# The mixer of a hybrid decoder: GpSimd's arithmetic goes to VectorE, and the cache's loads go from SyncE's queue to GpSimd's

## The chip, the core and the metric

One core of a Trainium2 chip runs the kernel. Its engines are TensorE (matrix products; "PE", its weight loads "PEld"), VectorE ("DVE"), ScalarE ("ACT"), GpSimd ("POOL") and SyncE ("SP", which in this kernel only issues transfers). Each engine executes its own queue in order; 16 DMA engines carry all transfers between the memory of the chip (HBM) and the on-chip memory (SBUF, 128 partitions). TensorE writes its sums to PSUM, which GpSimd cannot read. The metric is device time in microseconds (us) for one execution of the whole kernel, the median of several runs.

## The reference, cut to what matters

One layer of a hybrid decoder in float32, for a prompt of 256 tokens and, in the same pass, 8 decoded sequences ("batches") of 8 tokens each with a past of 2048 positions. All 320 tokens go through a half FFN, the mixer, and another half FFN.

```
h = ffn_half(x, ...)                              # x + 1/2 (silu(n Wg) * (n Wu)) Wd
z = rmsnorm(h) @ w_in                             # columns: q | k | v | a | b, 1024 each
q, k = rope(rmsnorm(q)), rope(rmsnorm(k))         # 16 heads of 64
u = a * sigmoid(b)
conv = silu(layernorm(causal_depthwise(u, 31 taps) + bias))
attn = mixture of 3 dilated windows: (128, every 1), (512, every 4), (2048, every 16)
h = h + concat(attn, conv) @ w_out
y = ffn_half(h, ...)
```

For the decoded tokens the attention reads keys and values from a cache of 2048 rows of 4 KB per batch; the windows need 512 near rows and, of the far ones, eight rows out of every sixteen. The conv of a decoded token reads 30 earlier rows of its state.

## The kernel before

**Layout.** Features lie on the partitions, the 320 tokens in the free dimension. A weight matrix is read in pieces of row tiles x 256 columns. Each piece is split in two for precision: wh, the high half (a cast on ScalarE, L238), and wl, the rest (raw - wh on VectorE, L239). `gemm` then runs three products per row tile, wh with the high half of the activations (L299), wh with the low half (L300), wl with the high half (L301). So TensorE can't finish a piece before ScalarE and VectorE have made its halves; there are three buffers for each half and four or five for the raw piece, which SyncE loads (L276) three pieces ahead in the mixer.

**Order.** The program is traced once, and a scheduler with a timing model of its own turns the trace into one fixed queue per engine. Work beside a gemm is traced between its pieces: `after` calls `pump`, which advances the attention of the decoded tokens (`sample`) by a fraction of a step per piece (RATE_K 0.55 beside the k products, RATE 1.05 beside conv and v, RATE_O 1.6 beside the output products), and takes NBG = 5 items per piece off `bg`, the conv's background list. `defer` traces something a few pieces later.

**Stages of the mixer.** q products; k products (the cache steps begin here); conv products c, four times two gemms (a and b); v products; the output projection's conv half with the prompt's attention beside it (o); then its attention half.

**Decoded tokens.** For each batch, `far_scores` takes six far tiles: it loads kf (128 cache rows x 1024, L511), multiplies it by qr, a copy of the batch's queries on all partitions (GpSimd, L512; qr is loaded at L507, one buffer), and sums each head's 64 products (VectorE, L513). `far_sums` spreads the sums with a mask (GpSimd, L520). `near_scores` loads four near tiles kn (L534), transposes them on TensorE and multiplies. `soft` is the softmax; its last steps are GpSimd's: z is cleared and filled (L568, L569) and px spread (L571). `values` loads ten value tiles vn (L610, VB = 3 buffers) and accumulates the products in PSUM (L614). kf has three buffers, kn two. All these loads are issued by SyncE, in the queue of the weights.

**Conv.** Per channel tile `conv_taps` lays 31 taps on `bg`: 21 on VectorE, each one instruction that multiplies and adds (L714 the first, L716 the others), and PTAPS = 10 as a product on ScalarE (L721, cprod) which GpSimd adds into csum (L725; the first is csum itself) and at the end to the rest (L749). `stap` does the decoded tokens in two halves: all windows times all taps on GpSimd (L734, into a buffer of kf), summed on VectorE (L736), the bias on ScalarE (L738). `norm_add` sums channel tiles, the even ones on VectorE, the odd ones on GpSimd (L808, L810); `act` halves its products in the same way (L839).

**q and k.** `qk_norm` runs two of its products on GpSimd (L447, L455) and GpSimd's copies to qsT and ksT (L458); conv's gate product is L791.

## Time and profile before

| | |
|---|---|
| median of 3 runs | 2650.08 us (2642.70 to 2655.48) |
| span of the profiled execution, from its first to its last instruction | 2650.1 us |
| instructions | 43147 |
| PE, PEld busy | 2536.2 us (96%), 2424.5 us (91%) |
| DVE busy | 1445.5 us (55%) |
| ACT busy | 1031.1 us (39%) |
| POOL busy | 447.6 us (17%), 392 instructions |
| DMA | 443.21 MB, 167 GB/s in the mean |
| cache loads | 80 vn, 48 kf, 32 kn, 512 KB each |

The profiled execution's own time is known as its span alone. A share of busy time is a mean over the whole span, in which FFN 1, the mixer and FFN 2 have different limits, so it is read by stage. "L301" is line 301 of the kernel; a group of instructions is named by its line, engine, operation and tiles (result <- operands). A wait is idle time of an engine, put down to what ended it. Matmuls are pipelined, and a busy PE isn't at its peak.

### The profile page before, as it was taken

The numbers are of one execution on the slowest core, as the hardware profiler recorded it, in microseconds if no ns is written. First come the engines' busy times: TensorE is split into PE (matmuls) and PEld (weight loads), VectorE is DVE, ScalarE is ACT, GpSimd is POOL, SyncE is SP. The second block draws the span as 40 slices with busy tenths as digits, with TensorE's granted clock in tenths as the row PEclk, the third lists the DMA queues.
The fourth block names the chain that finished last, engine by engine and source line by source line (L and its number), as shares of the span: only waits on it lengthen the run. The fifth ranks groups of instructions, "written<-read, shape, count | busy, mean of one in ns | idle before, by whom it ended". The sixth has DMA issues, their size and how long they took to land. (4 is left out here: it accounts for less than half of the span.)

```text
span 2650.1 us, 43147 instructions
## 1 busy us (share of the span) xinstructions
PE 2536.2 (96%) x17612; PEld 2424.5 (91%) x17612; DVE 1445.5 (55%) x1785; ACT 1031.1 (39%) x1597; POOL 447.6 (17%) x392
## 2 busy tenths in 40 slices
PE   7999999999999999888878899999999999999999
PEld 6999999999999998777666675999999999999999
DVE  5444444444444576979899744644444444444443
ACT  4333333333323456555434434533333333333333
POOL 3000000000000123746666400200000000000000
PEclk9999999999999999899989899999999999999999
DMA  6544444444444455978888966454444444544443
GB/s 191 162 151 151 147 149 151 151 151 149 149 149 151 151 156 166 237 217 232 232 216 232 259 186 185 146 153 150 151 152 148 151 149 149 151 151 150 148 150 119
DMA packets 385543, 443.21 MB, mean 167 GB/s; under 512 B 17274, under 2 KB 362290, under 8 KB 385328
## 3 DMA queue, kind: packets, MB, share of 16 engines
q1 hardware_dynamic: 385344, 440.45, 56.1%
q8 instruction: 138, 2.26, 0.4%
q14 instruction: 61, 0.50, 0.1%
HBM read 432.39 MB, written 8.71 MB: 166 GB/s over the span
## 5 line engine op out<-in xcount | busy, mean ns | idle before, releaser
L239 DVE TENSOR_TENSOR wl<-raw,wh 128x1024 fp32r<-128x1024 f32 (+1 forms) x736 | 868.6, 1182 | 933.9 <-ACT wh L238 921.7
L238 ACT CAST wh<-raw 128x1024 fp32r<-128x1024 f32 (+1 forms) x736 | 688.0, 936 | 1275.8 <-PE acc L300 1088.0
L299 PE MATMUL acc<-xh_a,wh 128*128 128x320 f32 x1408 | 437.2, 311 | 1.5 <-ACT wh L238 1.5
L300 PE MATMUL acc<-xl_a,wh 128*128 128x320 f32 x1408 | 437.4, 311 | 0.0
L301 PE MATMUL acc<-xh_a,wl 128*128 128x320 f32 x1408 | 436.9, 310 | 0.0
L301 PE MATMUL acc<-hh,wl 128*128 128x320 f32 x1408 | 435.5, 309 | 0.0
L299 PE MATMUL acc<-xh_c,wh 128*128 128x320 f32 x1408 | 435.3, 309 | 0.0
L300 PE MATMUL acc<-xl_c,wh 128*128 128x320 f32 x1408 | 435.1, 309 | 0.0
L301 PE MATMUL acc<-xh_c,wl 128*128 128x320 f32 x1408 | 435.1, 309 | 0.0
L300 PE MATMUL acc<-hl,wh 128*128 128x320 f32 x1408 | 435.0, 309 | 0.0
L299 PE MATMUL acc<-hh,wh 128*128 128x320 f32 x1408 | 435.0, 309 | 0.0
L348 POOL TENSOR_TENSOR hm<-ut,sg 128x320 f32<-128x320 f32 x88 | 77.4, 880 | 1659.5 <-DVE ut L346 1659.5
L299 PEld LDWEIGHTS acc<-xh_a,wh 128*128 128x128 f32 x1408 | 265.9, 189 | 1.7 <-ACT wh L238 1.6
L300 PEld LDWEIGHTS acc<-xl_a,wh 128*128 128x128 f32 x1408 | 266.0, 189 | 0.3 <-issue 0.2
L301 PEld LDWEIGHTS acc<-xh_a,wl 128*128 128x128 f32 x1408 | 265.8, 189 | 0.5 <-DVE wl L239 0.2
L300 PEld LDWEIGHTS acc<-xl_c,wh 128*128 128x128 f32 x1408 | 264.4, 188 | 0.1
L299 PEld LDWEIGHTS acc<-xh_c,wh 128*128 128x128 f32 x1408 | 264.4, 188 | 0.1
L301 PEld LDWEIGHTS acc<-xh_c,wl 128*128 128x128 f32 x1408 | 264.4, 188 | 0.0
L300 PEld LDWEIGHTS acc<-hl,wh 128*128 128x128 f32 x1408 | 264.3, 188 | 0.0
L301 PEld LDWEIGHTS acc<-hh,wl 128*128 128x128 f32 x1408 | 264.3, 188 | 0.0
L299 PEld LDWEIGHTS acc<-hh,wh 128*128 128x128 f32 x1408 | 264.2, 188 | 0.0
L301 PE MATMUL acc<-xh_b,wl 128*128 128x320 f32 x640 | 205.5, 335 | 42.3 <-DVE wl L239 42.3
(214 smaller groups left out, 3016.5 us busy)
## 6 DMA issues: line engine op xcount, KB each, us to landing
raw<-ffn_w_gate SPq DMA_DIRECT2D x176, 512.0 KB, 3.6
raw<-ffn_w_up SPq DMA_DIRECT2D x176, 512.0 KB, 3.5
raw<-ffn_w_down SPq DMA_DIRECT2D x176, 512.0 KB, 3.5
vn<-cache_v SPq DMA_DIRECT2D x80, 512.0 KB, 6.6
raw<-w_in SPq DMA_DIRECT2D x128, 256.0 KB, 4.6
kf<-cache_k SPq DMA_DIRECT2D x48, 512.0 KB, 8.7
kn<-cache_k SPq DMA_DIRECT2D x32, 512.0 KB, 6.8
raw<-w_out SPq DMA_DIRECT2D x64, 256.0 KB, 5.0
```

Source lines behind the costliest of these rows:

```text
L238: nc.scalar.copy(dsth, src)
L239: nc.vector.tensor_tensor(dstl, src, dsth.bitcast(F32), op=ALU.subtract)
L299: nc.tensor.matmul(a, h, hi[kk], start=st, stop=False)
L300: nc.tensor.matmul(a, h, lo[kk], start=False, stop=False)
L301: nc.tensor.matmul(a, l, hi[kk], start=False, stop=sp)
L348: nc.gpsimd.tensor_tensor(m, t, sg[j], op=ALU.mult)
```

## The change

In the mixer GpSimd computes nothing any more. Its products (cache rows by queries, L512; conv windows, L734; the spreads L520 and L571; q's and k's L447 and L455; the gate L791; half of the layer norm's) go to VectorE as they are. Of the conv's taps VectorE does 30 of 31, and the first (with the bias) goes to ScalarE; cprod, csum and their adds are gone. `norm_add` keeps one sum, on VectorE, and its first copy goes to ScalarE; so do the copies to qsT, ksT and z. z becomes two fixed buffers that are cleared once. GpSimd issues the loads of kf, kn and vn instead of SyncE; qr, the weights and all stores stay with SyncE. The conv's window products are put after taps 6 and 14 instead of 3 and 9. GpSimd's work in the FFNs (L176, L348) and a few clears are untouched.

```diff
-PTAPS = 10
...
-            nc.gpsimd.tensor_tensor(zq, zq, sd, op=ALU.mult)
+            nc.vector.tensor_tensor(zq, zq, sd, op=ALU.mult)
...
-            nc.gpsimd.tensor_tensor(rot, rot, sin, op=ALU.mult)
+            nc.vector.tensor_tensor(rot, rot, sin, op=ALU.mult)
...
-            nc.gpsimd.tensor_copy((qsT if is_q else ksT)[:, i, :], r[:, SEQ:T])
+            nc.scalar.copy((qsT if is_q else ksT)[:, i, :], r[:, SEQ:T])
...
+    zbuf = deque(sa.tile([P, 2 * TS - TD], F32, name=f"z{i}", bufs=1) for i in range(2))
+    for z in zbuf:
+        nc.vector.memset(z, 0.0)
...
     def far_scores(b, out):
...
-            nc.sync.dma_start(kn, rows(ck, b, n))
-            nc.gpsimd.tensor_tensor(kn, kn, qr, op=ALU.mult)
+            nc.gpsimd.dma_start(kn, rows(ck, b, n))
+            nc.vector.tensor_tensor(kn, kn, qr, op=ALU.mult)
...
-        nc.gpsimd.tensor_tensor(af, bc(sf), tmb, op=ALU.mult)
+        nc.vector.tensor_tensor(af, bc(sf), tmb, op=ALU.mult)
...
-            nc.sync.dma_start(kn, rows(ck, b, NFAR + n))
+            nc.gpsimd.dma_start(kn, rows(ck, b, NFAR + n))
...
-        z = sa.tile([P, 2 * TS - TD], F32, name="z")
-        nc.gpsimd.memset(z, 0.0)
-        nc.gpsimd.tensor_copy(z[:, TS - TD:TS], sm[:, SNEW:SFAR])
+        z = turn(zbuf)
+        nc.scalar.copy(z[:, TS - TD:TS], sm[:, SNEW:SFAR])
...
-        nc.gpsimd.tensor_tensor(px, bc(sm[:, SFAR:SW]), tmb, op=ALU.mult)
+        nc.vector.tensor_tensor(px, bc(sm[:, SFAR:SW]), tmb, op=ALU.mult)
...
-                nc.sync.dma_start(v, rows(cv, b, vrow[n]))
+                nc.gpsimd.dma_start(v, rows(cv, b, vrow[n]))
...
     def conv_taps(i, u):
...
             if j == 0:
-                nc.vector.tensor_scalar(ap, src, w, bias, op0=ALU.mult, op1=ALU.add)
+                nc.scalar.activation(ap, src, AF.Identity, bias=bias, scale=w)
             else:
                 nc.vector.scalar_tensor_tensor(ap, src, w, ap, op0=ALU.mult, op1=ALU.add)
 
-        def ptap(j):
-            first = "c" not in s2
-            t = turn(csum if first else cprod)[:, 0:SEQ]
-            nc.scalar.activation(t, u[:, j:j + SEQ], AF.Copy, bias=0.0, scale=dww[:, i, j:j + 1])
-            if first:
-                s2["c"] = t
-            else:
-                nc.gpsimd.tensor_tensor(s2["c"], s2["c"], t, op=ALU.add)
...
-            nc.gpsimd.tensor_tensor(pr4, win, w, op=ALU.mult)
+            nc.vector.tensor_tensor(pr4, win, w, op=ALU.mult)
...
-        nd = CW - PTAPS
-        for j in range(nd):
+        for j in range(CW):
             bg.append(lambda j=j: tap(j))
-            k = (j + 1) * PTAPS // nd - j * PTAPS // nd
-            for x in range(k):
-                bg.append(lambda x=j * PTAPS // nd + x: ptap(nd + x))
-            if j in (3, 9):
-                bg.append(lambda j=j: stap(j > 3))
-        def close():
-            nc.gpsimd.tensor_tensor(ap, ap, s2["c"], op=ALU.add)
-            norm_add("m", a, i)
-
-        bg.append(close)
+            if j in (6, 14):
+                bg.append(lambda j=j: stap(j > 6))
+        bg.append(lambda: norm_add("m", a, i))
...
-            nc.gpsimd.tensor_tensor(uc, at[j], t, op=ALU.mult)
+            nc.vector.tensor_tensor(uc, at[j], t, op=ALU.mult)
...
-        e = nc.gpsimd if i % 2 else nc.vector
-        k = key + str(i % 2)
-        if i < 2:
-            norm[k] = tmp.tile([P, T], F32, name="n" + k, tag=("ssa", "sd")[i % 2], bufs=1)
-            e.tensor_copy(norm[k], x)
+
+        if i == 0:
+            norm[key] = tmp.tile([P, T], F32, name="n" + key, tag="ssa", bufs=1)
+            nc.scalar.copy(norm[key], x)
         else:
-            e.tensor_tensor(norm[k], norm[k], x, op=ALU.add)
+            nc.vector.tensor_tensor(norm[key], norm[key], x, op=ALU.add)
...
-            (nc.gpsimd if i % 2 else nc.vector).tensor_tensor(cacc[i], cacc[i], s["r"], op=ALU.mult)
+            nc.vector.tensor_tensor(cacc[i], cacc[i], s["r"], op=ALU.mult)
```

## Rows read from the trace of the kernel before

**Rows 1.** The page's slices, TensorE: busy tenths, 40 equal slices of the span.
```profile
PE   7999999999999999888878899999999999999999
```

**Rows 2.** Stretches: length, busy us of PE, PEld, DVE, ACT, POOL, clock, DMA share, GB/s.
```profile
1024.00:1118.00 94.00, 82.69 (x533) 74.85 (x532) 74.37 (x73) 51.95 (x109) 55.04 (x39) 0.91 0.91 246
1118.00:1349.00 231.00, 195.16 (x1562) 163.00 (x1560) 205.17 (x262) 118.39 (x264) 144.44 (x121) 0.94 0.81 223
1349.00:1492.00 143.00, 109.26 (x812) 87.92 (x811) 123.57 (x144) 63.01 (x138) 85.30 (x59) 0.88 0.93 238
1492.00:1616.00 124.00, 117.79 (x901) 90.14 (x900) 67.17 (x159) 45.53 (x113) 17.98 (x12) 0.97 0.75 205
...
1437.00:1500.00 63.00, 48.05 (x324) 39.72 (x325) 45.91 (x54) 29.69 (x62) 33.63 (x20) 0.87 1.03 256
```

**Rows 3.** Waits of TensorE, 1024 to 1492: total us, times, longest.
```profile
PE acc L301 <- DVE wl L239: 42.3, 25, 4.7
```

**Rows 4.** Groups of VectorE, 1024 to 1492: xcount | busy us, mean ns | idle before, releasers.
```profile
L716 DVE SCALAR_TENSOR_TENSOR cacc<-u,dww,cacc 128x256 f32<-128x256 f32 x160 | 134.3, 867 | 0.6
L239 DVE TENSOR_TENSOR wl<-raw,wh 128x512 fp32r<-128x512 f32 x126 | 124.7, 996 | 22.7 <-ACT wh L238 20.7 <-ACT kt L497 2.0
...
L457 DVE TENSOR_TENSOR qk<-w,w 128x320 f32<-128x320 f32 x11 | 9.2, 839 | 1.7 <-POOL w L455 1.7
...
L714 DVE TENSOR_SCALAR cacc<-u,dww,gains 128x256 f32<-128x256 f32 x8 | 7.6, 944 | 2.1 <-ACT u L792 2.1
L839 DVE TENSOR_TENSOR cacc<-cacc,mu 128x320 f32<-128x320 f32 x4 | 5.1, 1321 | 0.0
```

**Rows 5.** Timeline of VectorE: start us, us, what; successive instructions overlap a little.
```profile
1222.68 1.26 DVE L716 SCALAR_TENSOR_TENSOR cacc<-u,dww,cacc 128x256 f32<-128x256 f32 x3
1223.86 0.68 DVE L239 TENSOR_TENSOR wl<-raw,wh 128x512 fp32r<-128x512 f32 x1
1224.46 1.26 DVE L716 SCALAR_TENSOR_TENSOR cacc<-u,dww,cacc 128x256 f32<-128x256 f32 x3
```

**Rows 6.** Timelines of GpSimd and VectorE, 1208 to 1227.
```profile
1208.40 2.37 POOL L512 TENSOR_TENSOR kf<-kf,qr 128x1024 f32<-128x1024 f32 x1
...
1208.90 2.16 DVE L716 SCALAR_TENSOR_TENSOR cacc<-u,dww,cacc 128x256 f32<-128x256 f32 x1
...
1226.81 0.91 POOL L749 TENSOR_TENSOR cacc<-cacc,csum 128x256 f32<-128x256 f32 x1 [5.93 <-DVE cacc L716]
```

**Rows 7.** Groups of VectorE, 200 to 800, in FFN 1.
```profile
L239 DVE TENSOR_TENSOR wl<-raw,wh 128x1024 fp32r<-128x1024 f32 x171 | 215.5, 1260 | 285.0 <-ACT wh L238 285.0
```

**Rows 8.** Groups of GpSimd, 1024 to 1492.
```profile
L512 POOL TENSOR_TENSOR kf<-kf,qr 128x1024 f32<-128x1024 f32 x43 | 109.2, 2545 | 60.1 <-DMA qr<-dqs 25.1 <-DMA kf<-cache_k 23.1 <-issue 4.2
...
L447 POOL TENSOR_TENSOR w<-w,w 128x320 f32<-128x320 f32 x10 | 10.7, 1072 | 11.0 <-DVE w L446 11.0
...
L839 POOL TENSOR_TENSOR cacc<-cacc,mu 128x320 f32<-128x320 f32 x4 | 4.6, 1166 | 0.0
```

**Rows 9.** Waits of VectorE, GpSimd and ScalarE, 1024 to 1492.
```profile
DVE wl L239 <- ACT wh L238: 20.7, 19, 4.7
DVE sf L513 <- POOL kf L512: 17.1, 7, 4.2
...
POOL kf L512 <- DMA qr<-dqs: 25.1, 4, 12.7
POOL kf L512 <- DMA kf<-cache_k: 23.1, 10, 5.0
...
ACT wh L238 <- DMA raw<-w_in: 50.8, 23, 7.1
...
ACT cacc L738 <- DVE cacc L736: 30.0, 8, 8.9
```

**Rows 10.** SyncE, 1024 to 1492: waits before issues; kf's issues, ns min/median/max.
```profile
SPq L276 <- DVE wl L239: 92.6, 56, 10.2
...
L511 SPq DMA_DIRECT2D kf<-cache_k x48: 536/542/640, 1024.6 to 1506.4; - x48
```

More of the change, by code (lines that the diff above doesn't have):

```diff
@@ L695, in block @@
     cp = cst.enter_context(tc.tile_pool(name="cp", bufs=2))
-    cprod = deque(cp.tile([P, 384], F32, name=f"cprod{i}", bufs=1) for i in range(3))
-    csum = deque(cp.tile([P, 384], F32, name=f"csum{i}", bufs=1) for i in range(2))
     srow = deque(cp.tile([120, 2, P], F32, name=f"srow{i}", bufs=1) for i in range(2))
@@ L708, in conv_taps @@
         ap, bias = a[:, 0:SEQ], gains[:, DWB + i:DWB + i + 1]
-        s2 = {}
         def tap(j):
@@ L802, in norm_add @@
     def norm_add(key, x, i):
-        e = nc.gpsimd if i % 2 else nc.vector
-        k = key + str(i % 2)
-        if i < 2:
-            norm[k] = tmp.tile([P, T], F32, name="n" + k, tag=("ssa", "sd")[i % 2], bufs=1)
-            e.tensor_copy(norm[k], x)
+        if i == 0:
+            norm[key] = tmp.tile([P, T], F32, name="n" + key, tag="ssa", bufs=1)
+            nc.scalar.copy(norm[key], x)
         else:
-            e.tensor_tensor(norm[k], norm[k], x, op=ALU.add)
+            nc.vector.tensor_tensor(norm[key], norm[key], x, op=ALU.add)
     def norm_mean(key):
         m = mtile("mu")
-        for i in range(2):
-            nc.tensor.matmul(m[:, 0:T], onesC, norm[key + str(i)], start=i == 0, stop=i == 1)
+        nc.tensor.matmul(m[:, 0:T], onesC, norm[key], start=True, stop=True)
         return m[:, 0:T]
```

## The prediction

> **What bounds the kernel now.** I read the page's slices first: TensorE shows 9 tenths nearly everywhere and thins out only in the middle [rows 1]. That is the mixer; both FFNs keep TensorE full, and the change does not enter them. I then cut the mixer where the products of the next gemm begin and read the busy times by stage [rows 2]: k products (1024 to 1118), conv products c (1118 to 1349), v products (1349 to 1492), attention beside the first output products o (1492 to 1616). In k, c and v TensorE is busy 387.1 of 468 us and its mean granted clock is 0.91, 0.94 and 0.88, so part of that time runs at the lower of its two levels, 1.2 instead of 2.4 GHz. VectorE is busy 74.4 + 205.2 + 123.6 = 403.2 of 468 us, the DMA engines for a share of 0.81 to 0.93 [rows 2]. The waits say which of the two ends last: TensorE's largest is for wl, the low half of a weight piece, which VectorE makes: 42.3 us in 25 waits [rows 3]. So from 1024 to 1492 VectorE's queue sets the pace, with the DMA engines close behind; in o it is busy 67 of 124 us and sets nothing.
>
> The reader should then see why VectorE is so busy. A conv tap (L716) takes 867 ns in the mean, a wl 996 ns [rows 4]. In a stretch in which GpSimd is silent (it idles 5.93 us up to 1226.81), three taps start to start take 1.18 us, 0.39 each, and a wl 0.60 us [rows 5, 6]. When a GpSimd product of two tiles runs, a tap of the same shape takes 2.16 us: it starts at 1208.90, half a microsecond into the product, and ends only after it [rows 6]. VectorE's two-input instructions stand still while GpSimd reads SBUF. GpSimd's help is paid for by VectorE.
>
> **Term 1, VectorE's work that goes (k to v).** Taps: 134.3 us busy less 160 x 0.40 = 64 gives 70. wl: 124.7 less 126 x 0.60 = 76 gives 49 [rows 4, 5]. L714, each tile's first tap, moves to ScalarE: 7.6. Six smaller two-input groups on 320 columns (L457 to L839 are the first and the last in [rows 4]; 39 instructions, 35.6 us) at 0.44 each, between a 256-column and a 512-column price, give 18. Together 145 us.
>
> **Term 2, VectorE's work that comes.** A two-input instruction of 1024 columns takes 1260 ns in FFN 1, where few meet GpSimd work [rows 7]; start to start I take 1.2. Then 43 cache products x 1.2 = 52; 16 window products of 992 columns x 1.17 = 19; 80 taps (ten of each of the eight channel tiles) x 0.40 = 32; 12 spreads of 768 columns (L520, L571) x 0.9 = 11; 40 of 320 columns (L447 and L839 are the first and the last of six groups) x 0.44 = 18 [rows 8]. Together 132 us. Net -13 us: VectorE does GpSimd's work in about the time that it now loses to GpSimd. Bounds: if only half of the taps' 70 came back, +22; if a straight line through the prices of 256 and 512 columns held up to 1024 (1.0 instead of 1.2, 59 products), -25.
>
> **Term 3, VectorE's idle time.** It is 468 - 403 = 65 us. 17.1 of it wait for a GpSimd cache product before the reduction [rows 9]; product and reduction now follow each other on one engine, so this goes. 20.7 wait for wh, which ScalarE makes [rows 9]. ScalarE is itself held up: 30.0 us behind a conv window whose product GpSimd makes late, 50.8 us for a weight load [rows 9]. The weights' queue on SyncE waits 92.6 us for a weight buffer, and each cache load that waits for its own buffer stands in front of the next weight [rows 10]. The loads of kf, kn and vn (160, each 0.54 us of SyncE [rows 10]) leave that queue, and ScalarE loses 80 tap products of its own while it gains 8 first taps and some small copies. I take two thirds of the 20.7, -14; bounds 0 and -20.7.
>
> The Trainium skill ("DMA: Bandwidth & Descriptors", section "Issuing engines are not separate DMA queues") speaks against this term: loads issued by any engine run on the same 16 DMA engines, and a second issuer saves only issue time. By it the -14 would be nothing and the time 2646 (which counts under E, below); I keep the row, because what it shows is an order of waits in one queue, not a lack of transfer rate.
>
> **Term 4, the new wait.** GpSimd absorbs today what VectorE will have to: 23.1 us for a kf row block to land and 25.1 us for qr, the queries' copy [rows 9]. VectorE executes in order, so behind such a wait stand wl (TensorE waits for that), taps and reductions. Ends: 0 and +48. kf loads no longer stand behind weights, so I take 8 of the 23; qr stays on SyncE with its single buffer, so I take 16 of the 25. +24.
>
> Sum for k to v: -13 - 17 - 14 + 24 = -20 us.
>
> **Term 5, the other stages.** The trace shows no load issued by GpSimd. Its cost lies between SyncE's issue, 0.54 us [rows 10], and GpSimd's longest common instruction, 2.5 us [rows 8]; it is nearer in kind to the first, so I take 1. In k to v buffers cover that, and 160 such issues are far below the stage's length. In o the last batch has 10 value tiles on three buffers, some three rounds on the path: +2, with ends 0 and +6. q (before 1024) keeps TensorE as its bound; its products, norm and rotation shorten a chain that nobody waits for there: 0. The memsets saved and two copies moved to ScalarE: 0, they lie beside waits.
>
> The sum is -18 us against the profiled execution's span of 2650.1 us, which equals the runs' median of 2650.08 us; what a run has outside the span isn't seen. **Forecast 2632 us.** The transfers allow it: k to v move 94 x 246 + 231 x 223 + 143 x 238 = 108.7 MB, in 448 us 243 GB/s, and the stretch 1437 to 1500 ran at 256 [rows 2].
>
> **Rivals.**
> *A, the forecast*: 2632, own range 2615 to 2648 (terms 2 to 4 vary together by half their bounds).
> *B, more is given back*: VectorE's queue, without instructions stretched to 2 us, keeps TensorE fed, no wait for kf or qr shows up, and transfers become the bound: 108.7 MB at 256 GB/s are 425 us instead of 468, with term 5 2609 us. For it: the wl wait is the largest one; against: 91% busy on VectorE and full DMA engines together.
> *C, slower: VectorE waits for loads*: all 48 us of GpSimd's waits go over and nothing of the 20.7 comes back: -13 - 17 + 48 + 2 = +20, 2670 us. It decides once VectorE's waits for kf and qr exceed 28 us (13 + 17 - 2). For it: an in-order engine, 86% busy, gets 43 new waits in front of wl; against: the loads' own queue.
> *D, slower: GpSimd can't issue fast enough*: the 160 loads are issued in some 616 us, 3.85 us each. If an issue costs 4.2 us, 160 x 4.2 = 672, +56, 2706 us; from 3.85 on it decides. Against: GpSimd's longest row plus one VectorE instruction of 1.2 us that it might have to wait for give 3.7.
> The Trainium skill has a rule of that kind ("SBUF — State Buffer", section "SBUF: two separate sides"): the descriptors of a DMA issued from GpSimd are written by GpSimd itself, which is locked out while VectorE runs in a 2-port mode. No run here shows it yet.
> *E, nothing to see*: DMA engines 0.81 to 0.93 busy are the real bound, and the terms only move waits: 2650.
>
> **How the numbers follow.** Within 0.5% (13 us) counts as the same, about what a measurement of this kernel can tell from no change. A 0.40 (0.26 faster, 0.14 same), B 0.17 (faster), C 0.22 (0.16 slower, 0.06 same), D 0.08 (slower), E 0.13 (0.02, 0.09, 0.02). Faster 0.45, same 0.29, slower 0.26. The range 2598 to 2688 takes in A, E, most of B and of C; the rest of B, the worst of C and D are left out, some 0.17.
>
> **What would show it.** Term 1: taps near 0.4 us apart and wl near 0.7 us in the mean, k to v. Term 2: VectorE's busy time between 1024 and the end of v near 390 us. Term 3: no wait for GpSimd, TensorE's wait for wl well below 42.3, ScalarE's for weights below 50.8. Term 4: VectorE's waits for kf and qr in the table of waits: 24 us; over 28, with nothing else given back, it is C. Term 5: GpSimd's time per issue, and loads issued later than buffers come free (D). The prediction is wrong at its root if VectorE is not what k to v wait for: then stage lengths stay although its waits change.

## The result and the profile after

The changed kernel takes 2688.1 us (median of 4 runs, 2684.6 to 2689.6) beside 2648.1 us for the kernel before: ratio 1.0138, 95% interval 1.0119 to 1.0157. It is slower by 40 us between the medians, or by 37 us as the ratio has it, where 2632 us and thus a gain of 18 was forecast; it lies just outside the range, whose upper end was 2688. That the range came so near is luck: it reached up there for rival C, which isn't what happened. The profiled execution has a span of 2682.9 us.

Where the time went is read from the same views as before. First the page's slices of the changed kernel: TensorE now has a hole in the middle, two slices of 3 and 5 tenths, and its granted clock falls to 6 tenths of full speed in the same two slices.

```profile
PE   7999999999999999799883599999999999999999
DVE  5444444444444577968879744744444444444443
...
PEclk9999999999999999899986698999999999999999
```

The stretches, cut where the products of the next stage begin (k, c, v, then the time from the last product of v to the first output product, which I call the gap, then o and the rest; columns as in [rows 2]):

```profile
1023.00:1125.00 102.00, 83.72 (x529) 74.84 (x529) 86.72 (x111) 51.74 (x115) 13.76 (x26) 0.91 0.85 236
1125.00:1335.00 210.00, 189.86 (x1568) 161.30 (x1567) 167.69 (x286) 100.70 (x223) 31.39 (x62) 0.96 0.89 246
1335.00:1476.00 141.00, 89.64 (x663) 78.70 (x662) 120.20 (x187) 37.01 (x76) 18.79 (x36) 0.81 0.81 211
1476.00:1518.00 42.00, 10.23 (x68) 5.31 (x66) 35.77 (x84) 11.59 (x25) 3.14 (x6) 0.63 0.36 99
1518.00:1652.00 134.00, 129.87 (x1037) 99.64 (x1038) 60.61 (x170) 55.76 (x140) 13.64 (x26) 0.96 0.67 193
1652.00:1684.00 32.00, 27.72 (x180) 14.19 (x179) 13.74 (x62) 13.29 (x44) 3.67 (x7) 0.79 0.52 135
```

Against [rows 2]: k 102 us (94 before), c 210 (231), v 141 (143), the gap 42 (none before: the first output product began as the last of v ended), o 134 (124). The last product of v ends at 1476, 16 us earlier than before; then TensorE is busy 10 of 42 us. VectorE's busy time up to the first output product is 410.4 us (403.2 before), so its work hardly grew. Its distribution did: in c it fell from 205 to 168 us, from the start of v to the first output product it rose from 124 to 156. TensorE's idle time shows where the loss lies, without work that only moved: 7 us more in k, 16 less in c, 18 more in v, 32 in the gap, 4 less in what follows.

The waits from 1023 to 1518 (total us, times, longest), of TensorE, VectorE, ScalarE and SyncE:

```profile
PE acc L298 <- DVE w L826: 34.0, 2, 27.1
PE misc_mu L793 <- DVE nm L789: 24.5, 1, 24.5
PE S L615 <- DMA vn<-cache_v: 24.0, 14, 4.6
PE acc L298 <- ACT wh L237: 18.0, 6, 5.2
PE acc L300 <- DVE wl L238: 6.6, 8, 1.6
...
DVE wl L238 <- ACT wh L237: 38.0, 27, 4.9
DVE kf L514 <- DMA kf<-cache_k: 21.8, 12, 4.8
...
DVE kf L514 <- DMA qr<-dqs: 0.9, 2, 0.6
...
ACT wh L237 <- PE acc L299: 93.3, 56, 8.3
ACT wh L237 <- DMA raw<-w_in: 63.9, 22, 9.0
ACT u L773 <- DVE cacc L714: 31.1, 2, 21.3
...
SPq L275 <- DVE wl L238: 133.8, 56, 22.0
```

And ScalarE's wait for a buffer of wh in the kernel before, 1024 to 1492:

```profile
ACT wh L238 <- PE acc L300: 34.9, 45, 2.5
```

TensorE's wait for wl is almost gone (6.6 us; 42.3 in [rows 3]). In its place stand two long ones: 27.1 us in v, once, for an evacuation (L826 empties the sums of v from PSUM; VectorE was busy 23.2 of those 27 us with what stood ahead of it), and 24.5 us for the layer norm's first sum, nm, to which VectorE adds the last channel tile late (L789). Its wait for value rows rose too, by less (24.0 us, 15.2 before). VectorE's wait for wh rose where it was to fall (38.0; 20.7 in [rows 9]). So did what holds ScalarE up before it makes wh: it waits for weights (63.9; 50.8), whose loads wait longer for a buffer that VectorE frees with wl (133.8; 92.6 in [rows 10]), and for a wh buffer that TensorE hasn't finished reading (93.3; 34.9).

The groups of VectorE from 1023 to 1518, then the taps in c alone, of the changed kernel; below them the issue of the far keys' loads (ns min/median/max):

```profile
L714 DVE SCALAR_TENSOR_TENSOR cacc<-u,dww,cacc 128x256 f32<-128x256 f32 x240 | 105.0, 478 | 0.0
L238 DVE TENSOR_TENSOR wl<-raw,wh 128x512 fp32r<-128x512 f32 x128 | 87.0, 686 | 38.1 <-ACT wh L237 38.0
L514 DVE TENSOR_TENSOR kf<-kf,qr 128x1024 f32<-128x1024 f32 x48 | 58.4, 1220 | 22.9 <-DMA kf<-cache_k 21.8 <-DMA qr<-dqs 0.9
...
L714 DVE SCALAR_TENSOR_TENSOR cacc<-u,dww,cacc 128x256 f32<-128x256 f32 x106 | 47.0, 479 | 0.0
...
L513 POOL DMA_DIRECT2D kf<-cache_k x48: 510/515/689, 1023.7 to 1459.6; - x48
```

And the taps in c of the kernel before, which [rows 4] has for the whole stretch only:

```profile
L716 DVE SCALAR_TENSOR_TENSOR cacc<-u,dww,cacc 128x256 f32<-128x256 f32 x117 | 92.7, 822 | 0.4
...
L714 DVE TENSOR_SCALAR cacc<-u,dww,gains 128x256 f32<-128x256 f32 x6 | 5.8, 964 | 2.1 <-ACT u L792 2.1
```

A tap now takes 478 ns (867 in [rows 4]), a wl 686 ns (996). But when c ended, 123 of VectorE's 168 taps were done before, and 106 of 240 now. The taps of a channel tile can't start before ScalarE has written its u. In the kernel before six tiles' u were written by the end of c and the last two at 1362 and 1365. In the changed kernel five were written by then, the sixth at 1359, and the last two only at 1445 and 1456, since the three u buffers were still held by taps that weren't done (start us, us, what, idle before and releaser):

```profile
1445.39 0.41 ACT L773 COPY u<-w 128x256 f32<-128x256 f32 x1 [21.28 <-DVE cacc L714]
...
1456.29 0.41 ACT L773 COPY u<-w 128x256 f32<-128x256 f32 x1 [9.87 <-DVE cacc L714]
```

So 123 of the 6 x 21 = 126 taps that could be done were done before, and 106 of 5 x 30 = 150 now, although a tap is cheaper and VectorE was idle 42 of 210 us.

The end of v on the timeline of the changed kernel, VectorE and then TensorE (start us, us, what, idle before and releaser):

```profile
1479.55 6.41 DVE L714 SCALAR_TENSOR_TENSOR cacc<-u,dww,cacc 128x256 f32<-128x256 f32 x16
...
1486.28 12.75 DVE L714 SCALAR_TENSOR_TENSOR cacc<-u,dww,cacc 128x256 f32<-128x256 f32 x32
...
1502.92 3.31 DVE L804 TENSOR_TENSOR cacc<-cacc,mu 128x320 f32<-128x320 f32 x8 [2.05 <-ACT mu L801]
1506.15 4.06 DVE L789 TENSOR_TENSOR nv<-nv,sq 128x320 f32<-128x320 f32 x7
1513.66 2.15 DVE L814 RECIPROCAL mu<-sd 128x320 f32<-128x320 f32 x1 [3.45 <-ACT sd L812]
1515.85 3.30 DVE L817 TENSOR_TENSOR cacc<-cacc,mu 128x320 f32<-128x320 f32 x8
...
1460.16 0.63 PE L298 MATMUL acc<-xh_b,wh 128*128 128x320 f32 x1 [27.09 <-DVE w L826]
...
1501.02 1.41 PE L793 MATMUL misc_mu<-nm,onesC 128*128 128x320 f32 x2 [24.51 <-DVE nm L789]
...
1518.09 0.56 PE L298 MATMUL acc<-ch,wh 128*128 128x320 f32 x2 [1.68 <-ACT ch L237]
```

The last 50 taps run back to back while TensorE stands, then the layer norm, 17.5 us in small steps between three engines; only then does the first output product have its operand. Before, the taps ended at 1434 and the layer norm ran beside products of v that TensorE still had.

### The profile page after: what moved, and what is told of

Its sections match the earlier page's. It is cut to its first block, busy times and chain, and to the rows that moved or that the text cites. A ratio compares the mean times of both kernels' runs of the same rounds, so it can differ in the third digit from the quotient of the medians.

```text
span 2682.9 us, 42903 instructions
## 1 busy us (share of the span) xinstructions
PE 2533.2 (94%) x17608; PEld 2426.3 (90%) x17608; DVE 1447.4 (54%) x1989; ACT 1008.3 (38%) x1551; POOL 214.1 (8%) x308
## 5 line engine op out<-in xcount | busy, mean ns | idle before, releaser
L238 DVE TENSOR_TENSOR wl<-raw,wh 128x1024 fp32r<-128x1024 f32 (+1 forms) x736 | 820.6, 1117 | 939.1 <-ACT wh L237 930.7
L298 PE MATMUL acc<-xh_b,wh 128*128 128x320 f32 x640 | 211.4, 332 | 54.1 <-DVE w L826 34.0
```

The lines of the kernel that those rows point to most:

```text
L238: nc.vector.tensor_tensor(dstl, src, dsth.bitcast(F32), op=ALU.subtract)
L298: nc.tensor.matmul(a, h, hi[kk], start=st, stop=False)
```

## The experiments

Theory 1, formed from this trace: the loss is no sum but a deadline. The output projection begins with the conv's half, VectorE reaches the end of the conv late, and TensorE has nothing else by then. Theory 2: a plain sum, every microsecond of VectorE's work from k on is paid. Theory 3 (the loads): queue, rate or wait. The recorded expectations use these numbers loosely (in e1 and e2 theory 2 is the loads' queue, in e4 theory 3 is the u buffers); what a number means there stands in the expectation itself. "e1" and so on are the runs' labels in short. e10, e11 and e21 leave work out and e18 loads a part of the keys only: they measure what something costs and are no versions to use.

| run | median us | kernel before, beside it | ratio (95%) | v + gap, us |
|---|---|---|---|---|
| the change | 2688.1 | 2648.1 | 1.0138 (1.0119 to 1.0157) | 141 + 42 |
| e1 loads on SyncE | 2695.5 | 2648.4 | 1.0156 (1.0127 to 1.0185) | 134 + 40 |
| e2 loads alone | 2717.5 | 2648.4 | 1.0241 (1.0212 to 1.0270) | 145 + 87 |
| e4 five u buffers | 2680.9 | 2648.4 | 1.0103 (1.0073 to 1.0132) | 115 + 55 |
| e5 keys' products back | 2700.1 | 2649.8 | 1.0193 (1.0165 to 1.0220) | 131 + 51 |
| e6 keys' products alone | 2673.3 | 2652.9 | 1.0076 (1.0058 to 1.0094) | 123 + 31 |
| e7 taps back | 2673.6 | 2648.4 | 1.0084 (1.0058 to 1.0109) | 111 + 46 |
| e10 21 taps | 2674.4 | 2652.9 | 1.0074 (1.0053 to 1.0096) | 111 + 51 |
| e11 no keys' products | 2667.0 | 2652.9 | 1.0051 (1.0032 to 1.0069) | 123 + 38 |
| e13 change, fewer sample steps | 2726.0 | 2649.8 | 1.0285 (1.0266 to 1.0303) | 125 + 42 |
| e14 two chains | 2675.6 | 2652.9 | 1.0089 (1.0071 to 1.0107) | 116 + 44 |
| e16 two chains, five u buffers, fewer sample steps | 2719.3 | 2649.8 | 1.0257 (1.0237 to 1.0276) | 106 + 43 |
| e17 kernel before, fewer sample steps | 2710.7 | 2649.8 | 1.0234 (1.0206 to 1.0261) | 106 + 39 |
| e18 small loads | 2669.5 | 2652.0 | 1.0059 (1.0042 to 1.0076) | 122 + 38 |
| e19 conv first | 2688.3 | 2652.0 | 1.0136 (1.0119 to 1.0154) | 112 + 57 |
| e20 two chains, five u buffers, 0.8 steps | 2694.7 | 2652.0 | 1.0161 (1.0146 to 1.0176) | 103 + 47 |
| e21 two chains, no keys' products | 2652.2 | 2652.8 | 0.9998 (0.9987 to 1.0009) | 106 + 25 |
| e22 two chains, keys' products on GpSimd | 2680.2 | 2652.8 | 1.0109 (1.0089 to 1.0129) | 132 + 24 |

### Which moved part costs: loads, products or taps

**e1**, the three cache loads of the changed kernel back on SyncE:
```diff
-            nc.gpsimd.dma_start(kn, rows(ck, b, n))
+            nc.sync.dma_start(kn, rows(ck, b, n))
```
(and the same for kn and vn).

> The changed kernel with one part undone: SyncE issues the loads of kf, kn and vn again; GpSimd computes nothing in the mixer. Theory 1 (VectorE's queue: too many taps are left when the v products end, and the norm follows them while TensorE has nothing to do): the hole of some 41 us at the end of v stays, 2675 to 2700 us. Theory 2 (the loads' new queue makes the loss: VectorE's 22 us for kf, TensorE's 24 us for vn): 2640 to 2660, and both waits fall to under 10 us.

Measured 2695.5 us, gap 40 us. Its interval overlaps the changed kernel's, so with GpSimd's arithmetic gone the queue that issues the loads makes no difference to the time that is clear of the noise. Theory 1 held, the loads' queue fell (VectorE still waits 19.9 us for kf). The waits do differ in the two traces: with the loads on SyncE VectorE waits 46.1 us for wh (38.0 in the change) and TensorE 21.2 us for wl (6.6).

**e2**, the kernel before with the three loads issued by GpSimd, the arithmetic where it was:
```diff
-            nc.sync.dma_start(kn, rows(ck, b, n))
+            nc.gpsimd.dma_start(kn, rows(ck, b, n))
```

> The kernel before with one part of the change alone: GpSimd issues the loads of kf, kn and vn beside its arithmetic. Theory 1: no hole at the end of v, 2640 to 2660 us, since VectorE's work is as before. Theory 2: slower by 20 us or more, 2670 or above.

A miss for theory 1: 2717.5 us, the slowest of these parts; theory 2's "2670 or above" held. From its waits of GpSimd and TensorE from 1023 to 1573:

```profile
POOL vn L610 <- PE S L614: 47.4, 19, 5.2
POOL kf L511 <- DVE sf L513: 17.7, 9, 6.3
...
PE misc_mu L815 <- POOL nm L810: 20.3, 1, 20.3
```

GpSimd works in order. Each load that waits for its buffer to come free (47.4 and 17.7 us) now stands in front of GpSimd's products and of the conv's sum nm, for which TensorE then waits 20.3 us, and 13.6 us for the second sum behind it. What fills the rest of this gap of 87 us stays open. The two halves of the change don't add up: loads alone cost 69 us (2717.5 less 2648.4), arithmetic alone 47 (e1), both together 40, each between medians.

**e6**, the kernel before with only the far keys' products on VectorE:
```diff
-            nc.gpsimd.tensor_tensor(kn, kn, qr, op=ALU.mult)
+            nc.vector.tensor_tensor(kn, kn, qr, op=ALU.mult)
```

> The kernel before with one part of the change: the 48 products of the far keys with q are made by VectorE; taps, sums and loads stay as before. Theory 1 (a deadline: what costs is the place of the last taps and of the conv's layer norm in VectorE's queue, behind the last evacuation of v): in this kernel all 168 of VectorE's taps stand ahead of the last evacuation of v, as before, so the gap between the last product of v and the first output product stays under 12 us (before about 0, after 42) and the time is 2648 to 2662. Theory 2 (a sum: every us of VectorE's work between k and the output projection is paid): 48 products at 1.22 us are 58 us more, less the 17.1 us wait for GpSimd's product and some 15 us of contention given back: 2670 to 2680.

2673.3 us and a gap of 31 us. Theory 1 in this form (no gap, since all taps stand ahead of the last evacuation in VectorE's queue) fell; the sum's 2670 to 2680 held. What stands in the gap is the layer norm, 13.7 us of it TensorE's wait for its second sum, with key products and reductions between its steps.

**e5**, the changed kernel with those products back on GpSimd (e6's diff in the other direction):
```diff
-            nc.vector.tensor_tensor(kn, kn, qr, op=ALU.mult)
+            nc.gpsimd.tensor_tensor(kn, kn, qr, op=ALU.mult)
```

> The changed kernel with one part undone: the 48 products of the far keys go back to GpSimd, taps, sums and everything else stay on VectorE. Theory 1 in its present form (TensorE has the same work, and what is lost is its idle time at the end of v while the conv's chain on VectorE ends: some 32 of the 42 us of the gap): VectorE loses 58 us of work, but its queue in v still holds some 40 taps behind the last evacuation, so a gap of 35 to 45 us stays and the time is 2664 to 2682, as for the kernel without these products (2667). Theory 2 (it was the products that did it, since the other moves only take contention away): no gap, 2640 to 2652.

A miss for both: 2700.1 us. GpSimd again has loads in front of its products (in its waits, vn 105.9 us, kf after the reduction 38.1 us), and VectorE's busy time up to the first output product rose by 17 us, to 427, though 58 us of products had left it: what remains there is dearer again.

**e7**, the changed kernel with 10 of the 31 taps back on ScalarE and GpSimd:
```diff
-        for j in range(CW):
+        nd = CW - PTAPS
+        for j in range(nd):
             bg.append(lambda j=j: tap(j))
...
+                bg.append(lambda x=j * PTAPS // nd + x: ptap(nd + x))
```

> The changed kernel with ten of the 31 taps of each tile back on ScalarE and GpSimd; cache products, window products and the rest stay on VectorE, the loads with GpSimd. Theory 1: 32 us of taps less on VectorE against some 40 us that taps and wl lose again beside GpSimd's adds, but only a dozen taps are left at the end of v, so the hole shrinks to 20 to 30 us: 2655 to 2675. Theory 2: no change against the changed kernel, 2680 to 2695.

2673.6 us, as expected, but the gap is 46 us and it is v that got shorter (111).

**e4**, five u buffers instead of three, because ScalarE waited 31.1 us for a u buffer:
```diff
-    ubuf = deque(cp.tile([P, UTOT], F32, name=f"u{i}", bufs=1) for i in range(3))
+    ubuf = deque(cp.tile([P, UTOT], F32, name=f"u{i}", bufs=1) for i in range(5))
```

> The changed kernel with five instead of three buffers for u, the conv's input. Theory 3 (ScalarE stands 31 us before a u buffer that the late taps hold, and behind it stand the weights' casts): those 31 us go, the hole shrinks by half or more, 2650 to 2668 us. Theory 1: the casts come sooner, but some 40 taps and the norm still follow the last v product, 2672 to 2688.

2680.9 us, in theory 1's range: v 26 us shorter, the gap 13 us longer. The last two u are now written at 1354 and 1382, and 122 taps instead of 106 are done when c ends. So the buffers hold part of the taps back, but only 7 us of the time.

### A sum or a position

**e10**, fewer taps:
```diff
-        for j in range(CW):
+        for j in range(CW - 10):
```

> The changed kernel with the last 10 of the 31 taps of each conv tile left out of the computation (80 fewer taps of 0.44 us, 35 us less of VectorE). Theory 1: 16 taps instead of 51 stand behind the last evacuation of v, so the gap ahead of the first output product falls from 42 to about 26 us and the time to 2668 to 2676. Theory 2: all 35 us come back, 2650 to 2658.

**e11**, no products of the far keys:
```diff
-            nc.vector.tensor_tensor(kn, kn, qr, op=ALU.mult)
```

> The changed kernel with the 48 products of the far keys with q left out of the computation (the reductions read the keys as loaded): 48 x 1.22 = 58 us less of VectorE, more than the 80 taps of the run beside it. Theory 1: 40 taps instead of 51 still stand behind the last evacuation of v, so the gap stays at 36 to 40 us, the stages k, c and v lose some 10 to 20 us, and the time is 2665 to 2680. Theory 2: the 58 us come back but for 10, 2630 to 2642.

e10 gained 14 us of its 35, e11 21 of its 58 (2674.4 and 2667.0 us). Both times lie in theory 1's ranges, and e11's gap of 38 us too; but e10's gap rose to 51 us where it was to fall to 26. So it is neither a sum nor a gap that shrinks with the taps behind it. The stretches of e11 (c, v, gap):

```profile
1133.00:1340.00 207.00, 186.60 (x1560) 158.83 (x1559) 152.55 (x272) 97.33 (x218) 31.50 (x62) 0.96 0.90 242
1340.00:1463.00 123.00, 87.83 (x666) 76.65 (x665) 96.84 (x171) 36.46 (x76) 18.26 (x35) 0.86 0.90 229
1463.00:1501.00 38.00, 10.33 (x67) 5.19 (x65) 32.21 (x74) 11.50 (x24) 3.14 (x6) 0.64 0.42 108
```

In c VectorE has 15 us less to do (152.6, after 167.7), and c is only 3 us shorter: VectorE isn't its bound. TensorE is busy 187 of 207 us there.

**e14** keeps the work and breaks the chain: a tile's taps go into two accumulators in turn.
```diff
+        bq = cp.tile([P, SEQ], F32, name="bq", bufs=3)
...
-                nc.vector.scalar_tensor_tensor(ap, src, w, ap, op0=ALU.mult, op1=ALU.add)
+                d = bq if j % 2 else ap
+                nc.vector.scalar_tensor_tensor(d, src, w, d, op0=ALU.mult, op1=ALU.add)
...
+        bg.append(lambda: nc.vector.tensor_tensor(ap, ap, bq, op=ALU.add))
```

> The changed kernel with the same conv work in another order: the 31 taps of a tile go into two accumulators in turn (one more product on ScalarE and one addition on VectorE for each tile, one tap less on VectorE), so that a tap needn't wait in the order for the one before it. 14 taps and two additions instead of 51 taps stand behind the last evacuation of v. VectorE's work is the same within 1 us. Theory 1: the gap falls from 42 to 24 to 30 us and the time to 2670 to 2680. Theory 2: the time stays at 2684 to 2692, the taps just lengthen c and v by what the gap loses.

2675.6 us; the time is theory 1's, the gap (44) isn't. Its taps in c, and its c, v and gap:

```profile
L718 DVE SCALAR_TENSOR_TENSOR cacc<-u,dww,cacc 128x256 f32<-128x256 f32 x73 | 33.5, 476 | 0.0
L718 DVE SCALAR_TENSOR_TENSOR bq<-u,dww,bq 128x256 f32<-128x256 f32 x68 | 31.1, 477 | 0.0
...
1134.00:1352.00 218.00, 194.39 (x1570) 164.05 (x1568) 183.94 (x328) 104.41 (x233) 32.01 (x64) 0.93 0.87 238
1352.00:1467.00 115.00, 89.15 (x658) 76.53 (x657) 100.32 (x168) 36.16 (x76) 15.71 (x30) 0.90 0.87 223
1467.00:1511.00 44.00, 11.23 (x71) 5.81 (x69) 38.67 (x62) 12.09 (x25) 6.20 (x12) 0.57 0.74 185
```

141 taps are done when c ends, not 106, and VectorE is busy 184 us in c, not 168; 139 us of its work are left for v and the gap, not 156. v and gap together take 159 us, not 183; k and c together took 15 us longer, so 9 us are left up to the first output product, and 12 in the time.

**e19** moves the place instead: two chains, five u buffers, the conv's steps 12 at a time (NBG) and ahead of the sample's, so that all taps and the layer norm stand ahead of the last evacuation of v in VectorE's queue:
```diff
-NBG = 5
+NBG = 12
...
-            bg_run(nb)
+            with tc.high_priority(HPB):
+                bg_run(nb)
```

> The changed kernel with two accumulators for the taps, five u buffers, and the conv's steps traced 12 instead of 5 at a time and ahead of the sample's, so that all taps and the whole layer norm stand ahead of the last evacuation of v in VectorE's queue: no VectorE work is left behind it (about 32 us in the changed kernel), but 55 us instead of 19 us stand ahead of it, behind the evacuation before. The sum is the same. Theory P (position: it matters that the conv ends before the products of v do): the gap is under 8 us, v at most 135, time 2645 to 2662. Theory S (from v on VectorE is the bound, so the gap only moves into v): v grows by what the gap loses, v and gap together stay at 155 to 170 us as with the two accumulators alone, time 2668 to 2680.

```profile
1345.00:1457.00 112.00, 87.07 (x610) 76.33 (x609) 108.26 (x185) 34.93 (x72) 14.63 (x28) 0.88 0.81 215
1457.00:1514.00 57.00, 16.39 (x130) 9.36 (x129) 42.73 (x67) 20.04 (x43) 6.85 (x14) 0.64 0.57 153
```

2688.3 us, outside both ranges: nothing gained. v and the gap still take 169 us with 151 us of VectorE's work in them. In v VectorE is busy 108 of 112 us; the products of v end on time and VectorE's queue doesn't. It even lost e14's gain, in part behind this stretch: the first output product comes 3 us later than in e14, and the output projection up to its attention half takes 6 us longer. Position alone isn't the cause; I gave up theory 1's "51 taps behind the evacuation" for theory S: TensorE sets the pace of c, and from v on VectorE does, for the work it has left by then plus the layer norm's steps.

### Are the loads late

**e18**, the changed kernel with the far keys' loads cut to a sixteenth, VectorE's work the same:
```diff
-            nc.gpsimd.dma_start(kn, rows(ck, b, n))
-            nc.vector.tensor_tensor(kn, kn, qr, op=ALU.mult)
+            nc.gpsimd.dma_start(kl, rows(ck, b, n)[:, :, 0:HD])
+            nc.vector.tensor_tensor(k3(kn), kl[:, None, :].to_broadcast([P, 16, HD]), k3(qr), op=ALU.mult)
```

> The changed kernel with the loads of the far keys cut to a sixteenth (64 of the 1024 columns; the products repeat them, so VectorE does the same 48 products and reductions of the same size on other data): 48 x 480 KB = 24 MB less on the way, about a fifth of what is loaded between k and the output projection. VectorE's work is unchanged. Theory L (VectorE's added idle time, above all the 38 us for ScalarE's casts of the weights and the 22 us for the keys, comes from loads that are late: k and c are bounded by the DMA engines): VectorE's idle time from k to the first output product falls from 85 to below 60 us, c to below 200, and the time to 2645 to 2665. Theory Q (it comes from the order of the queues alone, weights that TensorE has not yet freed and u buffers that the taps free late): the wait for the keys goes, the one for the casts stays above 30 us, c stays at 205 to 212, and the time is 2672 to 2686.

Its stretches c, v and gap, and VectorE's largest wait:

```profile
1134.00:1350.00 216.00, 193.78 (x1630) 161.48 (x1629) 168.64 (x287) 103.37 (x227) 33.10 (x65) 0.97 0.76 214
1350.00:1472.00 122.00, 88.19 (x602) 77.69 (x600) 115.57 (x188) 35.47 (x72) 15.55 (x30) 0.83 0.56 154
1472.00:1510.00 38.00, 10.74 (x67) 5.40 (x66) 32.15 (x74) 11.76 (x24) 3.16 (x6) 0.60 0.39 106
...
DVE wl L238 <- ACT wh L237: 40.1, 27, 4.9
```

The DMA share in c falls from 0.89 to 0.76, but c takes 216 us (210 in the change), VectorE still waits 40.1 us for wh, and 108 taps are done when c ends. So neither the pace of c nor VectorE's idle time in it comes from the load rate. That is theory Q's picture, though c is 4 us over its range (205 to 212) and its time (2672 to 2686) was missed by 2.5 us, since the wait for the keys' data (21.8 us) is gone and v is 19 us shorter, while VectorE's other waits and k took most of the rest back.

### Do the causes add up

**e21**: two chains (e14) and no keys' products (e11) together.

> The changed kernel with two accumulators for the taps, and with the 48 products of the far keys left out of the computation. Theory S (TensorE sets the pace of c and VectorE that of v and the gap, where it takes VectorE's work plus some 20 us of the layer norm's steps): v and gap together fall from 160 (two accumulators alone) and 161 (no products alone) to 128 to 140 us, the two gains of 12 and 20 us add up, time 2650 to 2660. If v and gap have a floor of their own instead (v was never under 102, the gap never under 38 with all taps on VectorE), they stay at 150 us or more and the time at 2663 to 2670.

```profile
1131.00:1356.00 225.00, 199.62 (x1630) 167.48 (x1629) 169.10 (x310) 103.31 (x231) 33.57 (x66) 0.92 0.87 236
1356.00:1462.00 106.00, 82.97 (x596) 72.14 (x595) 93.19 (x166) 34.95 (x72) 16.23 (x31) 0.92 0.95 240
1462.00:1487.00 25.00, 11.57 (x72) 6.06 (x72) 18.94 (x41) 11.68 (x24) 3.14 (x6) 0.66 0.63 169
```

2652.2 us, ratio 0.9998. VectorE has 112 us of work left for v and the gap, and these take 131 us, 19 more. The kernel before has 143 for 124 ([rows 2]), e19 169 for 151, e14 159 for 139, the changed kernel 183 for 156: a remainder of 18 to 27 us, for the layer norm's steps and VectorE's waits. It isn't the same everywhere: e18 has 12 (160 for 148), e11 32 (161 for 129), e10 33 (162 for 129), and the runs with fewer sample steps, below, 8 to 15. In e2, where TensorE waits for a sum that GpSimd makes, it is 71. But save for e2, v and the gap follow the work left for them over a span of some 50 us, with 8 to 33 us on top. e14's 12 us and e11's 21 add up to 33 of the 36 us between the medians of the changed kernel and of e21, whose time is that of the kernel before. The other side of it: only without the products does the changed kernel draw level.

**e22**: two chains, the products on GpSimd, the loads on SyncE (the diffs of e14, e5 and e1 together).

> The changed kernel with two accumulators for the taps, the 48 products of the far keys back on GpSimd and all cache loads back on SyncE: GpSimd keeps one job, without waits for buffers in front of it, VectorE has the rest. Theory S: VectorE loses 58 us of products and gets back some 20 to 25 us of contention and 10 to 15 us of waits for GpSimd, the gap falls to 15 to 30 us, time 2655 to 2668. If GpSimd's products cost VectorE no more than they take off it in v, 2640 to 2652.

A miss: 2680.2 us, no faster than e14. The gap is 24 us, but c takes 230 and v 132: VectorE's busy time up to the first output product is 428 us against e14's 409, although the 58 us of products are off it. The loads' queue isn't the reason (e1 has 412 us, the change 410): GpSimd's products cost VectorE more than they take off it.

### Moving the sample's work into the output projection

Four runs lowered RATE, the sample's steps for each piece of c and v: **e13** the changed kernel with 0.6, **e16** the same with two chains and five u buffers, **e17** the kernel before with 0.6, **e20** the changed kernel with 0.8, two chains, five u buffers and RATE_O 2.5.
```diff
-RATE = 1.05
+RATE = 0.6
```

> The changed kernel with one number changed: the sample attention goes forward 0.6 steps for each weight piece of c and v instead of 1.05, so that some 40% of its loads, of its products on TensorE and of its work on VectorE move from c and v into the output projection, where VectorE was busy 45% and the DMA engines 67%. Theory 1: TensorE's idle time in v and the gap falls, since the conv's chain shares VectorE with less; c about as long, the last tap 15 to 30 us earlier, the output projection 15 to 25 us longer, time 2668 to 2682. Theory 3 (c and v are bounded by the loads, 0.89 and 0.81 of the DMA engines' time): c and v shrink by 30 us or more together, the gap stays at 40 us, time 2655 to 2668.

> The changed kernel with the two accumulators of the taps, five u buffers and 0.6 steps together: each takes away one thing that holds the conv's chain up (the tap before it, the buffer, the sample's work in VectorE's queue). 6 taps stand behind the last evacuation of v. Theory 1: the gap falls below 25 us and the time to 2645 to 2662. Theory 3: as for the kernel with 0.6 steps alone, within 4 us.

> The kernel before with 0.6 steps instead of 1.05. Theory 1: it has no gap to lose, and the sample's work that moves into the output projection only makes that longer, where TensorE is busy 95%: 2650 to 2670. Theory 3: the loads that go from c and v into the output projection make it faster, 2630 to 2645.

> The changed kernel with two accumulators, five u buffers, 0.8 sample steps for each weight piece of c and v instead of 1.05, and 2.5 instead of 1.6 in the output projection, so that the sample attention still ends with it. Theory S: k to the first output product takes 460 to 472 us (448 with 0.6 steps, 486 with 1.05 and two accumulators), the output projection and the tail 170 to 185 instead of 166: 2655 to 2672. If the sample's chain is too slow for 2.5 steps (as with 0.6 and 1.6, where the tail was 120 us), the tail is 50 us or more and the time above 2680.

All were slower: 2726.0, 2719.3, 2710.7 and 2694.7 us, outside every range but one (e20's last sentence, a tail of 50 us or more and over 2680). k to the first output product fell to 456, 448, 458 and 470 us (495 for the change), but the attention half of the output projection then began only some 120, 120, 99 and 72 us after the products of its conv half (32 for the change), since the sample's attention ended late. And e17, with GpSimd's help and no gap before, has a gap of 39 us. These runs settle nothing about the cause; they show that the kernel before stood at a point from which a step in several directions (e2, e6, e17) opens a gap.

## Why the prediction was wrong

**Term 1** held: taps 0.40 us apart and 478 ns long, wl 686 ns as "near 0.7"; no VectorE instruction is stretched by GpSimd any more. **Term 2** held in its prices (1220 ns for a key product, 1.2 forecast). VectorE's busy time to the first output product is 410 instead of 403 us. By then it has five more key products and six more reductions behind it (48 against 43 and 42, at 1.22 and 1.21 us some 13 us), so like for like -6 where -13 was forecast.

**Term 3** is the first step that failed. The wait for GpSimd went, as said. The 20.7 us for wh were to shrink by 14; they became 38.0. The main reason given was that the cache loads leave the weights' queue. They left it, and that made 8 us of this wait (46.1 in e1, 38.0 without); what outweighs it comes with the moved arithmetic, which raises the wait from 20.7 to 46.1. In the time the loads' move made no difference that is clear of the noise. That agrees with the Trainium skill ("DMA: Bandwidth & Descriptors", section "Issuing engines are not separate DMA queues"), by which loads of any engine run on the same 16 DMA engines and a second issuer saves issue time alone. Nor were the weights late for lack of rate (e18), which speaks against rival E too. In c TensorE is the pace maker, busy 190 of 210 us; ScalarE waits for the wh buffers that it still reads (93.3 us instead of 34.9 from k to the first output product), VectorE meets each weight piece early and waits in order, and ready taps stand behind it.

**Term 4** held in its sum by luck: 21.8 + 0.9 = 22.7 us of new waits for kf and qr, 24 forecast, but kf was to take 8 of it and qr 16. So rival C, which decided at 28, didn't come about; the time is on its side for another reason. **Rival D** is wrong: GpSimd issues a load in 515 to 532 ns in the median, at most 689. The Trainium skill's rule beside it ("SBUF — State Buffer", section "SBUF: two separate sides") has GpSimd locked out of writing descriptors while VectorE runs in a 2-port mode. Beside a VectorE that is busy 85% of v this trace shows no such lock-out; in which mode VectorE's instructions ran no row says, so the rule itself isn't tested.

**The sum for k to v**, -20, seems to come close: the last product of v ends at 1476 instead of 1492. That is luck. What the sum adds up is VectorE's time, and up to the first output product that came to +27: its busy time +7 instead of -13, its idle time 85 us instead of 65 and so +20 instead of -7. Term 3's wait for wh alone makes 31 us of the difference (+17 instead of -14). **The step that failed is to end the sum at the last product of v.** It took the end of v's products for the end of VectorE's work, and let what VectorE gains in one stage count in the next. VectorE's busy time fell in c, where TensorE had no use for more speed, and rose by 32 us from v on, where VectorE is last; 36 us of it ran after the last product of v, with the layer norm's steps behind them. No rival contained a conv that ends late: I read in [rows 2, 3] that VectorE set the pace from 1024 to 1492 and did not ask what must be finished at 1492, nor what hid the layer norm. The prediction's last sentence named the sign of it (VectorE isn't what the stage waits for) and it was true of c. **Term 5** missed too: k took 8 us longer, o 10 (TensorE is busy 130 of 134 us there: small products of the sample that had been done earlier came later, above all 12.0 instead of 7.6 us of key transposes and 5.6 instead of 1.4 us of the far sums' products); the q stage is unchanged at 61 us.

How far the cause is shown: that VectorE's work left for v and the gap decides most of the loss is shown by e14, e11 and e21 together, with the spread of 8 to 33 us in what comes on top. That c leaves more taps undone because they are one serial chain of 30 on one engine, where 21 and 10 ran side by side on two before, is shown so far as two chains move 35 taps into c, and five u buffers 16; how the scheduler comes to lay the single chain so thinly was not tried. In k TensorE's wait for wh rose from 2.2 to 10.1 us, about what k lengthens by; why wh comes later there stays open. A version that beats the kernel before wasn't found.

## What to carry to other kernels

Add up an engine's work by stage and up to the deadline of what it feeds, not over the whole stretch: time that it gains in a stage where another engine sets the pace can't be saved up for the stage where it is last itself. Before a helper engine's arithmetic is taken away because it slows its neighbour, ask what ran side by side with it: here ten of the 31 taps back on the helpers (e7) gained as much as ten taps left out (e10), 14 us each, and the same taps in two chains on one engine (e14) gained 12 us at equal work. And before loads go to another engine's queue, list what that engine must still compute behind a load that waits for its buffer (e2: 69 us).

## What the runs showed of the hardware

- Beside GpSimd's arithmetic VectorE's two-input instructions took longer in the kernel before, 867 ns for a tap and 996 ns for a wl in the mean; without any GpSimd arithmetic they take 478 and 686 ns. With only the 48 key products back on GpSimd (e22) the taps of the two chains take 661 and 602 ns, the wl 826 ns.
- That contention was nearly worth its price: VectorE does all of GpSimd's work in 7 us more than what it did before, and the kernel is no faster for it.
- A load of kf (512 KB) issued by GpSimd occupied it 515 ns (SyncE: 542 ns, [rows 10]), one of vn 527 and one of kn 532 ns, and kf's loads landed in 6.7 us in the median (8.7 before).
- In the gap, where TensorE did next to nothing, its granted clock was 0.63, after 0.81 in v and ahead of 0.96 in the next stage: part of that time at 1.2, the rest at 2.4 GHz. TensorE's busy time from k to the end of the mixer is the same as before all the same (531.0 and 532.6 us), so the clock explains none of the loss: what grew is TensorE's idle time there, from 93 to 130 us.
